# The opening of a fused encoder layer: where a constant part is summed, what stands ahead of the norm's root, and which engine does the sine products

## The chip, the cores and the metric

The kernel runs on one core of a Trainium2 chip. The metric is the device time of one execution in microseconds; less is better. Five engines take part: TensorE (PE in the profile; its weight loads are PEld), VectorE (DVE), ScalarE (ACT), GpSimd (POOL) and SyncE (SP), whose queue issues nearly all the transfers. Each engine works through its own instructions strictly in the order in which they stand; semaphores tie the engines together. A wait at the head of one engine therefore holds everything that is queued behind it there.

## The reference

One layer over 1024 positions of 1024 features, in float32:

```
mod = silu(c) @ w_ada + b_ada
sh1, sc1, g1, sh2, sc2, g2 = split(mod, 6)
h = rms_norm(x, norm_mix_g) * (1 + sc1) + sh1
q_a, k_a, v_a, qk_m, v_m, o_m, gates = split(h @ w_in)
y_attn = axial_gqa_attention(rope(rms_norm(q_a)), rope(rms_norm(k_a)), v_a)
y_mem  = bidirectional_mlstm(silu(conv(qk_m)), v_m, o_m, gates)
x = x + g1 * (concat(y_attn, y_mem) @ w_out)
h = rms_norm(x, norm_ffn_g) * (1 + sc2) + sh2
x = x + g2 * ((silu(h @ w_gate) * (h @ w_up)) @ w_down)
return rms_norm(x, final_norm_g)
```

Attention has 8 query heads of 64 and 2 key heads; the rope turns pairs by cosine and sine tables. The mLSTM has 4 heads of 128 and sixteen gate columns, from which running maxima and sums over all positions are made.

## The kernel before

**Tiles.** Features lie on the partitions: x is eight blocks of 128 x 1024 (`x_t`), cut into two halves of 512 positions. Every large product is done as three matmuls (`mm3`, lines 307 to 310): each operand is split into a rounded part (hi) and the rest (lo), and hi x hi, hi x lo and lo x hi are added. The hi part is made on ScalarE (`whi`, `hh`), the lo part on GpSimd or VectorE (`wlo`, `hl`).

**Who sets the order.** The program is written by a planner (`Clock`): it keeps estimated times of the engines, a heap of pending steps, and chains of steps that wait for flags. Each instruction is emitted when its step comes up, so the order on every engine is a result of these estimates and fixed before the run. The chip then follows that order with its true times.

**The opening.** It runs in these stages:

1. *First batch* (line 670 on): while x arrives, three weight tiles (key, value, first query; `acc0`) are multiplied with x scaled by `sc1` alone, without the norm's root and without the shift. Beside it VectorE multiplies rows of `w_ada` with the conditioning (`ada_load`): eight scale columns first, then eight shift columns a0 to a7. The squares of x are summed, and after step k = 5 the norm's root is made (`rstd_steps`, line 603): a table function on ScalarE, then a correction on VectorE, two halves. `rstd` is copied into PSUM (`ms`) by ScalarE.
2. *Second batch* (line 2046 on): now `h_steps` (line 656) makes h itself: x times root (VectorE), scale and shift (ScalarE), hi (ScalarE), lo (GpSimd). With h, PE does the first token-major tile (gates and v of the mLSTM, `acct`, 272 columns, `chunk_step`) and the second query tile (`query`): half 0, then half 1; in half 1 the query products come after the tile's.
3. *Shift's part.* Key, value and first query lack the shift's product with their weights. `load_again` fetches these weights once more, and `shift_sums` multiplies them with the shift (24 tiny products). When it is there, `shifted` finishes the three tiles on ScalarE.
4. *Ropes.* `rope_steps` (line 706): the swapped rows are moved by four transfers (`swap`), multiplied with the sine table (`rp[1]`) on GpSimd, the tile with the cosine table on VectorE, then added. The key's ones need the roots of the key's squares as well; each query has one group of tiny products for its squares.
5. *Gates* (`gate_steps`, line 926): the gate columns (`gI`) are turned by PE into rows, through log-sigmoid on ScalarE, four scans and some ten row operations on VectorE, exponentials on ScalarE, back into columns by PE (the T products of line 1024), and a last sum (`dexp`, line 1042).

From there on PE works through the other projection tiles (`units`), which are also the filling beside attention. Attention begins when queries and gates are done; its scores are S (line 1104). After it come the mLSTM, the output projection and the feed-forward part, which the change doesn't touch.

**Names in the rows.** `ada`: a column of `w_ada` (128x1024) or half a column (128x512, `ada_late`); `sq<-ms`, `sq<-sq`: the root's steps; `wst`, `whi`, `wlo`: a weight piece as it came, its hi and its lo; `raw_q`: the first batch's tiles as they are finished; `sqk`: squares of such a tile; `sw`: the swapped rows; `rps`: the rope tables; `gs`, `gI`: gate columns; `gt`, `Fr`, `T`, `gB`, `rend`: rows of the gates' chain; `wagain`: the weights fetched again. Big buffers of the pool `bp` (tag `big`) are a ring of five.

Of the kernel before, what the change touches and what calls it, by code (L numbers as in the profile page):

```python
# [20 lines left out]
P = 128  # L21
# [226 lines left out]
def layer_kernel(ctx, tc, xT, c, w_ada, vecs, cons, rope, w_f, w_t0, w_t, w_o, w_gu, w_d, out):  # L248
# [112 lines left out]
    with tc.manual_schedule():  # L361
# [122 lines left out]
        def load_piece():  # L484
# [8 lines left out]
            if isinstance(specs[i][0], str):  # L493
# [3 lines left out]
                  lo=dve if specs[i][3:] == (1,) or i < 6 or start["m", 2] <= i < start["b", 1] else None)  # L497
# [28 lines left out]
        ck.at(3.0, lambda: dve.tensor_scalar(b1, V("b_ada", 8, KT), 1.0, None, op0=OP.add))  # L526
        x_at = [Flag() for _ in range(KT)]
        ada_at = [Flag() for _ in range(16)]
        sq_ok, z_ok = {}, {}
        z_read = [Flag() for _ in range(KT)]  # L530
# [21 lines left out]
        def ada_load(j):  # L552
            t = bp.tile([P, D], F32, tag="big", name="ada")
            ck.chain(dma(t, w_ada[j]), *([*z_ok[7], *sq_ok[7]] if j < 8 else []), lambda: dve.scalar_tensor_tensor(
                t, t, 1.0, PP["cond"], op0=OP.mult, op1=OP.mult, accum_out=modacc[:, 0, j:j + 1]), flag=ada_at[j])
# [62 lines left out]
        def shift_sums():  # L618

            ck.need(y_free, slot("ms").flag())  # L620
            acc, f = psum_tile([P, 3, 2], "ms")
# [17 lines left out]
        wagain, again = {}, {}  # L639

        def load_again():

            gI[0] = stp.tile([P, NJ, 2, 64], F32, tag="x", name="gI", bufs=KT)
            gps.memset(gI[0], 0.0)
            for i in range(3):
                w = wagain[i] = stp.tile([P, S], F32, tag="x", name="wagain", bufs=KT)
                again[i] = ck.chain(dma(w, w_f[i].rearrange("p a b -> p (a b)")), lambda: None)
            for i in range(2):
                rp.append(stp.tile([P, S], F32, tag="x", name="rps", bufs=KT))
                dma(rp[i], rope[i])  # L650
# [5 lines left out]
        def h_steps(n, k, *after):  # L656
# [3 lines left out]
                0.0, *after, sh_ok[k], y_ok[n], z_read[k],  # L660
                lambda: dve.tensor_mul(xs, xs, msp[n][0]),
# [8 lines left out]
        for k in range(KT):  # L670
# [15 lines left out]
            if k == 5:  # L686
# [11 lines left out]
                ck.chain(0.0, *last[-3:], lambda: None, flag=y_free)  # L698

# [6 lines left out]
        def rope_steps(i, accs, raw=None, qg=None):  # L706
# [30 lines left out]
            def swap():  # L737
# [3 lines left out]
                ck.chain(arrive, lambda: gps.tensor_mul(sw, sw, rp[1]), lambda: dve.tensor_mul(qg, qg, rp[0]),  # L741
# [46 lines left out]
            else:  # L788
                ck.chain(0.0, rstd_ok[0], lambda: rooted(0), rstd_ok[1], lambda: rooted(1), shift_ok,
# [1252 lines left out]
        for _ in range(3):  # L2042
            load_piece()
        ck.chain(0.0, *sh_ok, lambda: act.activation(sh2, mod[:, 0:KT, None].to_broadcast([P, KT, 2]), AF.Copy), y_free,
                 load_again)
        accs, tiles = [], []
        for n in range(NH):
# [16 lines left out]
            for k in range(KT):  # L2064
# [4 lines left out]
                elif k % 2:  # L2069
                    load_piece()  # L2070
            for j in range(4 * n, 4 * n + 4):
                chunk_out(0, j, *tiles[j])
            if n:
# [182 lines left out]
```

## Time and profile before

| | us |
|---|---|
| three runs | 1399.79, 1400.19, 1396.09; median 1399.79 |
| the profiled execution | 1401.04 |
| its span, first to last instruction | 1399.2 |
| busy: PE, DVE, ACT, POOL | 1291.9, 1051.6, 674.6, 655.8 |
| mean granted clock of PE | 0.96 |

The page's second part shows the span in 40 slices of 35 us; digits are tenths. These are the rows of PE, of VectorE and of PE's granted clock:

```profile
PE   7799848999999999899798899999999999979997
DVE  7906998977888757777598887666766654898866
PEclk9898869999999999999899899999999999989998
```

The opening is the first six slices. PE is at its least in the sixth (175 to 210 us: 4 tenths, at a clock of 6 tenths), while VectorE is full there; in the third (70 to 105 us) it is the other way round. PE is close to full afterwards.

### The profile page before, as it was taken

Reading aid. Unit: us, or ns where it says so; the run is one execution under the profiler, and the core shown is the slowest. Engines: PE = TensorE matmul, PEld = TensorE weight load, DVE = VectorE, ACT = ScalarE, POOL = GpSimd, SP = SyncE. Lnnn points to the kernel's source line nnn. Section 1 sums busy time; section 2 is a strip of 40 time slices with the busy share of each in tenths; the row PEclk is TensorE's granted clock in tenths of the full one; section 3 lists DMA queues with packets and bytes.
Section 4 is the critical chain, followed back from the end, with each engine's and each line's share of the span. In section 5 each row is a group of like instructions: output and inputs, shape, how many; then the busy total and the mean of one; then the engine's idle time right before and its main releaser. Section 6 shows DMA issues by size and latency. Waiting matters only on the chain.

```text
span 1399.2 us, 19615 instructions
## 1 busy us (share of the span) xinstructions
PE 1291.9 (92%) x6632; PEld 1087.9 (78%) x6640; DVE 1051.6 (75%) x1615; ACT 674.6 (48%) x1217; POOL 655.8 (47%) x545
## 2 busy tenths in 40 slices
PE   7799848999999999899798899999999999979997
PEld 5698637888879888787586688888888887867887
DVE  7906998977888757777598887666766654898866
ACT  6746225666666655454376333323333333444462
POOL 0555724435444335786502255545545455545542
PEclk9898869999999999999899899999999999989998
DMA  9343534333112137833463242323322258733324
GB/s 355 122 164 108 165 118 115 116 110 110 52 54 61 35 112 228 281 124 106 158 200 98 83 158 91 108 104 113 113 96 85 83 175 320 295 83 100 97 64 155
DMA packets 103893, 185.99 MB, mean 133 GB/s; under 512 B 11376, under 2 KB 33136, under 8 KB 103792
## 3 DMA queue, kind: packets, MB, share of 16 engines
q1 hardware_dynamic: 90400, 162.63, 36.4%
q10 hardware_dynamic: 13392, 22.10, 4.1%
q8 instruction: 53, 0.87, 0.3%
q14 instruction: 48, 0.39, 0.1%
HBM read 137.76 MB, written 43.25 MB: 129 GB/s over the span
## 4 chain that ended last, share of the span: by engine, by line
PE 61%; DVE 20%; DMA 6%; issue 5%; ACT 4%; POOL 2%; SPq 1%; DVEq 0%; ACTq 0%; POOLq 0%
PE acc L308 15%; PE acc L309 15%; PE acc L310 15%; PE av L1155 3%; PE T L1136 2%; DVE sst L96 2%; PE S L1104 2%; DVE x L96 2%; DVE y L96 2%; DVE PT L96 2%; DVE ada L96 2%; PE acct L308 2%; PE acct L310 1%; PE acct L309 1%; DVE s L96 1%
## 5 line engine op out<-in xcount | busy, mean ns | idle before, releaser
L96 POOL TENSOR_TENSOR wlo<-wst,whi 128x512 fp32r<-128x512 f32 (+2 forms) x190 | 269.6, 1426 | 343.1 <-ACT whi L96 307.5
L96 ACT ACTIVATE whi<-wst 128x512 fp32r<-128x512 f32 (+2 forms) x219 | 131.1, 605 | 127.5 <-PE acc L310 31.9
L96 POOL TENSOR_SCALAR P<-P,sst 128x1024 f32<-128x1024 f32 x64 | 86.9, 1360 | 158.1 <-DVE sst L96 127.2
L309 PE MATMUL acc<-x,whi 128*128 128x512 f32 x352 | 138.7, 394 | 5.9 <-DVE x L96 5.9
L96 POOL TENSOR_TENSOR wlo<-wr,whi 128x512 fp32r<-128x512 f32 x56 | 77.5, 1385 | 75.4 <-ACT whi L96 74.0
L308 PE MATMUL acc<-whi,wch 128*128 128x512 f32 x244 | 96.5, 395 | 5.3 <-ACT wch L96 5.3
L308 PE MATMUL acc<-hh,whi 128*128 128x512 f32 x224 | 97.0, 433 | 3.4 <-ACT xp L96 1.9
L310 PE MATMUL acc<-whi,wcl 128*128 128x512 f32 x244 | 96.4, 395 | 2.9 <-DVE wcl L96 2.9
L309 PE MATMUL acc<-wlo,wch 128*128 128x512 f32 x244 | 96.4, 395 | 0.1
L96 ACT ACTIVATE P<-S,sst,colq 128x1024 f32<-128x1024 f32 x64 | 77.3, 1207 | 35.2 <-DVE sst L96 33.6
L96 ACT ACTIVATE PT<-T 128x512 fp32r<-128x512 f32 x128 | 71.9, 596 | 40.4 <-PE T L1136 39.8
L309 PE MATMUL acc<-hl,whi 128*128 128x512 f32 x224 | 90.7, 405 | 0.0
L310 PE MATMUL acc<-hh,wlo 128*128 128x512 f32 x224 | 90.6, 404 | 0.0
L96 DVE TENSOR_TENSOR PT<-T,PT 128x512 fp32r<-128x512 f32 x128 | 83.0, 682 | 9.1 <-ACT PT L96 8.7
L96 ACT ACTIVATE whi<-wr 128x512 fp32r<-128x512 f32 x60 | 37.9, 632 | 105.3 <-DVE wr L96 50.4
L308 PE MATMUL acct<-whi,hh 128*128 128x256 f32 (+1 forms) x256 | 79.1, 309 | 10.1 <-ACT hh L96 7.4
L96 DVE TENSOR_TENSOR sg<-acc,sg 128x512 f32<-128x512 f32 x67 | 45.4, 687 | 55.7 <-PE acc L310 55.5
L96 POOL TENSOR_TENSOR wlo<-s,whi 128x512 fp32r<-128x512 f32 x40 | 53.9, 1350 | 67.2 <-ACT whi L96 67.2
L309 PEld LDWEIGHTS acc<-x,whi 128*128 128x128 f32 x352 | 66.8, 190 | 21.0 <-DVE x L96 7.3
L96 DVE TENSOR_REDUCE sst<-S 128x1 f32<-128x1024 f32 x64 | 77.7, 1215 | 5.9 <-PE S L1104 5.9
L96 DVE SCALAR_TENSOR_TENSOR ada<-ada,cond 128x512 f32<-128x512 f32 (+1 forms) x80 | 70.5, 888 | 15.4 <-DMA ada<-in_w_ada_dram 9.5
L96 DVE TENSOR_TENSOR wcl<-wd,wch 128x512 fp32r<-128x512 f32 x50 | 50.7, 1025 | 37.8 <-ACT wch L96 32.1
(472 smaller groups left out, 3815.4 us busy)
## 6 DMA issues: line engine op xcount, KB each, us to landing
wr<-in_w_gu_dram SPq DMA_DIRECT2D x66, 256.0 KB, 2.9
ada<-in_w_ada_dram SPq DMA_DIRECT2D x64, 256.0 KB, 3.1
wd<-in_w_d_dram SPq DMA_DIRECT2D x22, 512.0 KB, 6.7
wst<-in_w_gu_dram SPq DMA_DIRECT2D x34, 256.0 KB, 3.1
wst<-act_d SPq DMA_DIRECT2D x33, 256.0 KB, 4.1
ada<-in_w_ada_dram SPq DMA_DIRECT2D x16, 512.0 KB, 6.9
wst<-in_w_o_dram SPq DMA_DIRECT2D x32, 256.0 KB, 3.3
act_d<-sg ACTq DMA_DIRECT2D x31, 256.0 KB, 2.0
```

What stands on the lines that cost most here:

```text
L96: return fn(*args, **kw)
L308: nc.tensor.matmul(acc, w[0], x[0], start=first, stop=False)
L309: nc.tensor.matmul(acc, w[0], x[1], start=False, stop=False)
L310: nc.tensor.matmul(acc, w[1], x[0], start=False, stop=last)
L1104: nc.tensor.matmul(sp[:, halves(n)], qs[:, j * P:(j + 1) * P], k2[g][m][:, halves(n)], start=m == 0, stop=m == 1)
L1136: nc.tensor.transpose(tp[:, k], Pt[q][:, (4 * b + k) * P:(4 * b + k + 1) * P], ident)
L1155: nc.tensor.matmul(av, va[:, k, h // 4], PT[it][m][:, k], start=(k, m) == (0, 0), stop=(k, m) == (NJ - 1, 1))
```

## The change

The diff has six parts:

- `shift_sums` is called between the two halves of the second batch, in a buffer of tag `acc`; `load_again` fetches the weights into big buffers as soon as the shift's columns are there, and the rope tables have a function of their own, `load_tables`, which waits as before until x is free.
- The shift columns a4 to a7 wait until the norm's root is done (`late`). A throw-away call loads the root's table early (`warm`). The first two x blocks take the root itself, not its copy in PSUM, and each block waits for its shift column only before the step that adds it.
- Weight pieces 6 to 8 are split on VectorE, not on GpSimd.
- The second query's `rope_steps` is set up after half 0, with a flag (`more`) for its second half; ropes, value transposes and gates now come in beside half 1. `gate_steps` is put in ahead of half 1's query products.
- The sine products go from GpSimd to VectorE, for all five ropes; they wait for the tables by a flag (`rp_ok`).
- Half columns of `w_ada` (`ada_late`) are asked for in every step of the second batch, and the second PSUM layout `ps0b` (four buffers for the small tags instead of two) is gone.

```
-                  lo=dve if specs[i][3:] == (1,) or i < 6 or start["m", 2] <= i < start["b", 1] else None)
+                  lo=dve if specs[i][3:] == (1,) or i < 9 or start["m", 2] <= i < start["b", 1] else None)
...
+        warm = stp.tile([P, 1], F32, name="warm")
+        ck.at(7.0, lambda: act.activation(warm, eps, AF.Abs_reciprocal_sqrt, scale=1.0, bias=eps))
...
-            ck.chain(dma(t, w_ada[j]), *([*z_ok[7], *sq_ok[7]] if j < 8 else []), lambda: dve.scalar_tensor_tensor(
+            ck.chain(dma(t, w_ada[j]), *([*z_ok[7], *sq_ok[7]] if j < 8 else []), *([late] if 3 < j < 8 else []), lambda: dve.scalar_tensor_tensor(
...
-            ck.need(y_free, slot("ms").flag())
-            acc, f = psum_tile([P, 3, 2], "ms")
+            ck.need(slot("acc").flag())
+            acc, f = psum_tile([P, 3, 2], "acc")
...
         def load_again():
 
+            for i in range(3):
+                w = wagain[i] = bp.tile([P, S], F32, tag="big", name="wagain")
+                again[i] = ck.chain(dma(w, w_f[i].rearrange("p a b -> p (a b)")), lambda: None)
+
+        def load_tables():
+
             gI[0] = stp.tile([P, NJ, 2, 64], F32, tag="x", name="gI", bufs=KT)
             gps.memset(gI[0], 0.0)
-            for i in range(3):
-                w = wagain[i] = stp.tile([P, S], F32, tag="x", name="wagain", bufs=KT)
-                again[i] = ck.chain(dma(w, w_f[i].rearrange("p a b -> p (a b)")), lambda: None)
             for i in range(2):
                 rp.append(stp.tile([P, S], F32, tag="x", name="rps", bufs=KT))
-                dma(rp[i], rope[i])
+                arrive = dma(rp[i], rope[i])
+            ck.chain(arrive, lambda: None, flag=rp_ok)
...
-                0.0, *after, sh_ok[k], y_ok[n], z_read[k],
-                lambda: dve.tensor_mul(xs, xs, msp[n][0]),
+                0.0, *after, (rstd_ok if k < 2 else y_ok)[n], z_read[k],
+                lambda: dve.tensor_mul(xs, xs, rstd[n] if k < 2 else msp[n][0]), sh_ok[k],
...
+                ck.chain(0.0, *rstd_ok, lambda: None, flag=late)
...
-                ck.chain(arrive, lambda: gps.tensor_mul(sw, sw, rp[1]), lambda: dve.tensor_mul(qg, qg, rp[0]),
+                ck.chain(arrive, rp_ok, lambda: dve.tensor_mul(sw, sw, rp[1]), lambda: dve.tensor_mul(qg, qg, rp[0]),
...
-                ck.chain(0.0, rstd_ok[0], lambda: rooted(0), rstd_ok[1], lambda: rooted(1), shift_ok,
+                ck.chain(0.0, rstd_ok[0], lambda: rooted(0), rstd_ok[1], more, lambda: rooted(1), shift_ok,
...
-        ck.chain(0.0, *sh_ok, lambda: act.activation(sh2, mod[:, 0:KT, None].to_broadcast([P, KT, 2]), AF.Copy), y_free,
-                 load_again)
+        ck.chain(0.0, *sh_ok, lambda: act.activation(sh2, mod[:, 0:KT, None].to_broadcast([P, KT, 2]), AF.Copy), load_again)
+        ck.chain(0.0, y_free, load_tables)
...
+                ada_late()
             for j in range(4 * n, 4 * n + 4):
                 chunk_out(0, j, *tiles[j])
-            if n:
+            if n == 0:
+                more = Flag()
+                rope_steps(1, accs, -1, raw_q[1], more)
+                while not again:
+                    ck.pop()
+                shift_sums()
+            else:
+                ck.chain(0.0, *vo_ok[0], gate_steps)
                 for k in range(KT):
                     query(k)
                     if k % 4 == 3:
                         load_piece()
-        rope_steps(1, accs, -1, raw_q[1])
-        while not again:
-            ck.pop()
-        shift_sums()
-        ck.need(*[f for ring in PP["ring"].values() for f in ring])
-        psum_open("ps0b", {"acc": ("acc", 4), "acct": ("acc", 4), "ms": ("aux", 4), "tr": ("aux", 4), "T": ("aux", 4)})
+                    ada_late()
+                more.set(ck, ck.t)
...
-        ck.chain(0.0, *vo_ok[0], gate_steps)
```

How the planner's order changes is seen at three places. First PE, where the shift's part is summed (`L626` before, `L629` now). Before, these rows follow the last query product of half 1:

```order
L310 MATMUL acc<-hh_229,wlo 128x512
L626 MATMUL ms<-sh_264,wagain 128x2 x24
L308 MATMUL acc<-hh_222,whi 128x512
L309 MATMUL acc<-hl_230,whi 128x512
L310 MATMUL acc<-hh_222,wlo 128x512
L938 MATMUL T<-ident,gI 128x128 x4
L308 MATMUL acc<-hh_223,whi 128x512
L309 MATMUL acc<-hl_231,whi 128x512
L310 MATMUL acc<-hh_223,wlo 128x512
L799 MATMUL tr<-ident,vt 128x128 x8
L938 MATMUL T<-ident,gI 128x128 x4
```

With the change they follow the last query product of half 0, and half 1 of the tile (`acct`) comes behind them:

```order
L308 MATMUL acc<-hh_229,whi 128x512
L309 MATMUL acc<-hl_237,whi 128x512
L310 MATMUL acc<-hh_229,wlo 128x512
L629 MATMUL acc<-sh_264,wagain 128x2 x24
L308 MATMUL acct<-whi,hh_222 128x272
L309 MATMUL acct<-wlo,hh_222 128x272
L310 MATMUL acct<-whi,hl_230 128x272
```

The sums moved ahead of 32 products into `acct` and 8 into `acc`. Behind them there follow, inside those 32, the value transposes (after 6), the key's squares and the first query's group (after 13 more) and the key's second half (after 5 more); the gates' first transposes come after 6 of the 8 query products. Up to the first scores S PE has 136 products into `acc` instead of 138, and VectorE 45 `ada` instructions instead of 35.

Second VectorE at the norm's root. Before, with the eight shift columns (`ada`) around the root's steps (`sq`):

```order
L96 SCALAR_TENSOR_TENSOR ada,modacc<-ada,cond 128x1024 x4
L96 TENSOR_SCALAR sq<-ms 128x512 x2
L96 SCALAR_TENSOR_TENSOR ada,modacc<-ada,cond 128x1024 x3
L96 SCALAR_TENSOR_TENSOR sq<-sq,ms 128x512 x2
L96 SCALAR_TENSOR_TENSOR ada,modacc<-ada,cond 128x1024
L96 SCALAR_TENSOR_TENSOR sq<-sq 128x512 x2
L96 TENSOR_TENSOR vt<-acc,sq 128x512
```

With the change:

```order
L96 SCALAR_TENSOR_TENSOR ada,modacc<-ada,cond 128x1024 x4
L96 TENSOR_TENSOR wlo<-wst,whi 128x544
L96 TENSOR_SCALAR sq<-ms 128x512 x2
L96 TENSOR_TENSOR wlo<-wst,whi 128x512
L96 TENSOR_TENSOR wlo<-wst,whi 128x544
L96 SCALAR_TENSOR_TENSOR sq<-sq,ms 128x512 x2
L96 SCALAR_TENSOR_TENSOR sq<-sq 128x512 x2
L96 TENSOR_TENSOR x_248<-x_248,sq 128x512
L96 TENSOR_TENSOR x_249<-x_249,sq 128x512
L96 TENSOR_TENSOR x_250<-x_250,ms 128x512
L96 SCALAR_TENSOR_TENSOR ada,modacc<-ada,cond 128x1024 x4
```

The late four columns moved behind the first three x blocks, and three weight splits came in.

Third VectorE at the gates. Before, from the last gate columns (`gs`) to the value tile (`va`):

```order
L96 COPY gs<-acct 128x16 x8
L96 COPY shift<-ms 128x3
L96 COPY gI<-gs 128x16x4 x2
L96 CAST maskb<-masks 128x128 x4
L96 TENSOR_SCALAR T_1106<-T,vec 64x512
L96 TENSOR_SCALAR Fr<-T,vec 64x512
L96 TENSOR_SCALAR T_1106<-T,vec 64x512
L96 TENSOR_SCALAR Fr<-T,vec 64x512
L96 SCALAR_TENSOR_TENSOR ada,modacc<-ada,cond 128x512 x2
L96 TENSOR_SCALAR sq<-ms 128x512
L96 TENSOR_TENSOR va<-tr,va 128x8x64 x2
```

With the change, up to the same gate columns (`raw_q_259` is the key, `raw_q_257` the first query):

```order
L96 TENSOR_TENSOR sw<-sw,rps 128x1024
L96 TENSOR_TENSOR raw_q_259<-raw_q_259,sw 128x1024
L96 SCALAR_TENSOR_TENSOR ada,modacc<-ada,cond 128x512
L96 TENSOR_SCALAR colq<-rqv 128x8x2
L96 SCALAR_TENSOR_TENSOR sq<-sq,ms 128x512
L96 TENSOR_TENSOR raw_q_257<-raw_q_257,rps 128x1024
L96 SCALAR_TENSOR_TENSOR ada,modacc<-ada,cond 128x512
L96 COPY gs<-acct 128x16 x4
L96 SCALAR_TENSOR_TENSOR sq<-sq 128x512
L96 TENSOR_TENSOR raw_q_257<-raw_q_257,sw 128x1024
L96 COPY gI<-gs 128x16x4 x2
L96 SCALAR_TENSOR_TENSOR ada,modacc<-ada,cond 128x512
```

Before, the ropes came behind the gates' first rows; now those of the key and the first query, sine products included, stand ahead of them.

More of the change, by code (lines that the diff above doesn't have):

```diff
@@ L529, in layer_kernel @@
         sq_ok, z_ok = {}, {}
+        late = Flag()
         z_read = [Flag() for _ in range(KT)]
@@ L639, in layer_kernel @@
         wagain, again = {}, {}
+        rp_ok = Flag()
         def load_again():
+            for i in range(3):
+                w = wagain[i] = bp.tile([P, S], F32, tag="big", name="wagain")
+                again[i] = ck.chain(dma(w, w_f[i].rearrange("p a b -> p (a b)")), lambda: None)
+        def load_tables():
             gI[0] = stp.tile([P, NJ, 2, 64], F32, tag="x", name="gI", bufs=KT)
             gps.memset(gI[0], 0.0)
-            for i in range(3):
-                w = wagain[i] = stp.tile([P, S], F32, tag="x", name="wagain", bufs=KT)
-                again[i] = ck.chain(dma(w, w_f[i].rearrange("p a b -> p (a b)")), lambda: None)
             for i in range(2):
                 rp.append(stp.tile([P, S], F32, tag="x", name="rps", bufs=KT))
-                dma(rp[i], rope[i])
+                arrive = dma(rp[i], rope[i])
+            ck.chain(arrive, lambda: None, flag=rp_ok)
         acc0 = [[psum_tile([P, HALF], "acc") for _ in range(NH)] for _ in range(3)]
@@ L704, in layer_kernel, with rope_steps @@
         va_ok = [Flag(), Flag()]
-        def rope_steps(i, accs, raw=None, qg=None):
+        def rope_steps(i, accs, raw=None, qg=None, more=FREE):
             is_k = i == 4
```

## The prediction

> **What bounds the kernel now.** I read the busy time by stage first, then who made TensorE (PE) wait, then its rows in order of time. Columns of the stages: start:end, length, busy time (count) of PE, PE's weight loads, VectorE (DVE), ScalarE (ACT), GpSimd (POOL), then PE's granted clock, DMA share, GB/s.
>
> ```profile
> 53.40:80.60 27.20, 19.24 (x111) 17.75 (x111) 15.44 (x26) 23.47 (x38) 22.65 (x18) 0.81 0.00 1
> ...
> 150.90:180.90 30.00, 24.68 (x97) 20.45 (x97) 29.69 (x32) 8.48 (x13) 17.95 (x9) 0.84 0.50 157
> 180.90:209.60 28.70, 14.22 (x49) 11.09 (x50) 26.22 (x43) 8.60 (x12) 8.07 (x6) 0.59 0.39 122
> 209.60:505.00 295.40, 281.20 (x1853) 249.66 (x1851) 250.83 (x439) 190.89 (x335) 126.31 (x96) 0.99 0.27 79
> ```
>
> From 209.6 us on PE is busy 95% at full clock: what comes later starts earlier if this point comes earlier. Before it PE stands still and then runs at a lower clock, while VectorE is full (29.69 of 30.00). The waits from 53 to 210 us (total, times, longest):
>
> ```profile
> PE T L1024 <- ACT T L96: 11.0, 2, 5.8
> PE acct L308 <- ACT hh L96: 7.4, 1, 7.4
> PE T L1042 <- DVE dexp L96: 7.3, 1, 7.3
> PE ms L754 <- ACT sqk L96: 6.4, 1, 6.4
> ```
>
> That is 32.1 us of standing still: 7.4 where the second batch begins (it waits for the root of the norm), 18.3 for the gates' tables, 6.4 for a query's squares. PE's own rows (start, duration, what; a wait in brackets):
>
> ```profile
> 60.91 0.59 PE L308 MATMUL acct<-whi,hh 128*128 128x272 f32 x1 [7.41 <-ACT hh L96]
> ...
> 65.14 0.63 PE L309 MATMUL acc<-hl,whi 128*128 128x512 f32 x1
> ...
> 67.96 0.29 PE L308 MATMUL acct<-whi,hh 128*128 128x272 f32 x1
> ...
> 68.34 0.40 PE L308 MATMUL acc<-hh,whi 128*128 128x512 f32 x1
> ...
> 69.04 0.29 PE L308 MATMUL acct<-whi,hh 128*128 128x272 f32 x1
> ...
> 99.84 8.26 PE L626 MATMUL ms<-sh,wagain 128*128 128x2 f32 x48
> 108.44 0.76 PE L308 MATMUL acc<-hh,whi 128*128 128x512 f32 x1 [0.34 <-DVE shift L96]
> ...
> 120.45 3.63 PE L754 MATMUL ms<-con,sqk 128*128 128x2 f32 x32
> ...
> 209.58 1.98 PE L1104 MATMUL S<-k,qs 128*128 128x512 f32 x8
> ```
>
> A product (three matmuls) takes 0.38 us into acct and 0.70 into acc (67.96, 68.34, 69.04; I use 0.68, their steady pace). After the 7.4 us wait a matmul takes 0.63 instead of 0.40 until about 67.9; after the tiny shift sums it is 0.76 as well. One group of squares (L754, half of its row) takes 1.75. Attention's first scores S start at 209.58: that is the mark I carry through.
>
> **The change, part by part.** *Opening.* These rows make the wait at 60.91:
>
> ```profile
> 41.77 2.38 DVE L96 SCALAR_TENSOR_TENSOR ada<-ada,cond 128x1024 f32<-128x1024 f32 x1
> ...
> 47.44 1.28 DVE L96 TENSOR_SCALAR sq<-ms 128x512 f32<-128x512 f32 x2
> ...
> 48.64 1.21 DVE L96 SCALAR_TENSOR_TENSOR ada<-ada,cond 128x1024 f32<-128x1024 f32 x1
> ...
> 54.41 1.28 DVE L96 SCALAR_TENSOR_TENSOR sq<-sq 128x512 f32<-128x512 f32 x2
> ...
> 57.41 1.86 DVE L96 TENSOR_TENSOR x<-x,ms 128x512 f32<-128x512 f32 x3
> ...
> 44.56 1.28 ACT L96 ACT_TABLE_LOAD   x1 [3.88 <-PE ms L690]
> ...
> 58.12 2.23 ACT L96 ACTIVATE x<-x,mod,sc 128x512 f32<-128x512 f32 x3
> ...
> 60.25 1.65 ACT L96 ACTIVATE hh<-x 128x512 fp32r<-128x512 f32 x3
> ...
> 40.24 5.04 POOL L96 TENSOR_TENSOR wlo<-wst,whi 128x544 fp32r<-128x544 f32 x2 [39.82 <-ACT whi L96]
> ...
> 60.94 18.78 POOL L96 TENSOR_TENSOR hl<-x,hh 128x512 fp32r<-128x512 f32 x15
> ```
>
> VectorE's root ends at 55.7 (54.41 + 1.28). Two of the first four shift columns took about 2.3 us instead of 1.2 while GpSimd split weights (41.77 beside 40.24); with pieces 6 to 8 split on VectorE that is 2.2 less, and one split (0.6, as an x product of that size: 1.86 / 3) more, ahead of the root: its first step goes from 47.4 to 45.9. Behind it four late columns leave (4 x 1.15 = 4.6) and two splits come (1.2), so the 8.25 us from there to the root's end become 4.85: **50.8**. The table load (1.28) is then done long before, in ScalarE's idle time near 8 us, hidden by PE's warm-up products; uncovered it would cost its 1.3. The first two x blocks take the root straight, so x is scaled by 51.5, two affine steps (0.74 each) and the first hh (0.6) end at **53.7**, where PE is just free (60.91 - 7.41 = 53.5).
>
> The gain isn't the whole 7.2: GpSimd's first hl takes 1.25 (18.78 / 15), so PE's third matmul waits 0.9, and three splits (3.8 us) now stand between its third and fourth hl, which costs PE 1.5 at the fourth group. Eight groups of 4 x 0.38 + 0.68 = 2.2 end the first half at 73.8, against 80.6 in the stages: **-6.8**. If the root didn't come earlier, this term is nil; if no producer held PE it is -9.
>
> *Sums between the halves.* Their 8.26 us stay on PE, with the slow matmuls after them (2.5 us), at 73.8 to 82.1. On SyncE's queue the three weight loads go ahead of the stores of v and of the rope tables, behind the second batch's weights; they need buffers that the late columns a4 to a6 free near 56, and have 17 us to land while the DMA engines stand empty (share 0.00). If they landed late, PE would wait there with the whole half queued behind it. The half columns of w_ada that are now fetched in each step of the batch cost VectorE 0.68 each, in a stage where it is busy for 15.44 of 27.20 and then nearly idle. What the new place does: v's transposes, the key's squares and one query's group (about 4 us of PE) come inside the half's 32 products of 0.38, and their VectorE work runs where VectorE idled. PE then reaches the gates' transposes at 82.1 + 2.5 + 12.2 + 4 + 6 x 0.68 = 105. VectorE hands over the gate columns only behind the ropes of key and first query: their 25 instructions, 0.2 to 1.2 us each, start when the shift is there (82.4) and end at 106.5, waits for the swapped rows included. So PE waits 1.5 there, and the gates start only 2 us sooner than now. Queued behind them on VectorE are the ropes of the later queries.
>
> *Gates' tables and sine products.* VectorE and GpSimd now:
>
> ```profile
> 108.24 0.30 DVE L96 COPY gI<-gs 128x64 f32<-128x64 f32 x2
> ...
> 128.43 1.23 DVE L96 TENSOR_TENSOR raw_q<-raw_q,sw 128x1024 f32<-128x1024 f32 x1
> ...
> 132.77 3.38 DVE L96 SCALAR_TENSOR_TENSOR Fr<-Fr,gt 64x1024 f32<-64x1024 f32 x1
> ...
> 136.08 0.68 DVE L96 SCALAR_TENSOR_TENSOR ada<-ada,cond 128x512 f32<-128x512 f32 x1
> ...
> 143.08 0.70 DVE L96 SCALAR_TENSOR_TENSOR ada<-ada,cond 128x512 f32<-128x512 f32 x1
> ...
> 147.05 3.29 DVE L96 TENSOR_TENSOR raw_q<-raw_q,sw 128x1024 f32<-128x1024 f32 x1
> ...
> 150.37 2.28 DVE L96 TENSOR_TENSOR_SCAN T<-Fr,T 32x1024 f32<-32x1024 f32 x1
> ...
> 167.45 4.60 DVE L96 COPY rend<-gB 32x8 f32<-32x8 f32 x2
> ...
> 178.56 1.21 DVE L96 TENSOR_TENSOR Fr<-gB,mprev 64x1024 f32<-64x1024 f32 x1
> ...
> 127.57 1.06 ACT L96 ACTIVATE gt<-gt 64x1024 f32<-64x1024 f32 x1
> ...
> 116.63 2.42 POOL L96 TENSOR_TENSOR sw<-sw,rps 128x1024 f32<-128x1024 f32 x1 [9.35 <-DMA sw<-raw_q]
> ...
> 129.90 5.17 POOL L96 TENSOR_TENSOR sw<-sw,rps 128x1024 f32<-128x1024 f32 x2
> ...
> 166.48 5.55 POOL L96 TENSOR_TENSOR k<-kdup,k 128x1024 fp32r<-128x1024 f32 x2
> ```
>
> From gI (108.24) to the logarithm's end (128.63) it is 20.4 us, broken by the key's roots on ScalarE; those now come first, and three passes of the query, abs, exp, log and two loads (about 12 us behind the transposed gates) put the logarithm's end at 119. From the first Fr (132.77) to the last (179.77) VectorE is full for 47.0. Out of these go the 7.0 from 136.08 to 143.08 (key and first query, done earlier) and what GpSimd's sine products took from VectorE: 2.2 in Fr (3.38 beside 129.90's row), 2.1 at 147.05 (clean: 1.23, at 128.43) and about 1.5 later, 5.8 in all; one sine product (1.2) comes in. 47.0 - 7.0 - 5.8 + 1.2 = 35.4: the last Fr ends at 119 + 35.4 = **154.5** instead of 179.8. PE gets there with 55 products (37.4), three groups (5.3) and 1 from 106.5, at 150.
>
> What remains collides still: two 32x8 copies took 4.60 beside 166.48's row. Without any collision the stretch is 28 us: four scans of 2.28, eleven operations of 1.2, six half columns of 0.68, some 2 of small ones. That is the lower end; the upper end, 10 us over mine, has each GpSimd subtraction left there hold VectorE for all its time.
>
> The Trainium skill, "SBUF — State Buffer", section "Who interferes with whom", has it that a VectorE operation with two SBUF inputs and a GpSimd one that reads SBUF exclude each other for a whole instruction. By that rule the moved products only change who waits, and five splits (1.25) and two key subtractions (2.8) would hold VectorE some 12 us above the clean 28: the last Fr at 159, and a sum 4.5 us higher, inside the forecast's own range. The trace agrees as far as 167.45 beside 166.48 goes.
>
> From the last Fr to S it is now 209.6 - 179.8 = 29.8, with two waits on the way (the second T and dexp). Six products now stand between the columns and dexp's sum, eleven behind it instead of ten: I take 26 (bounds 23 and 30). S starts at 180.5: **-29.1** (of which the opening is 6.8). By then two projection products fewer are done (136 against 138): **+1.4**. Without the second PSUM layout the transposes share two buffers instead of four until attention: that parts the T transposes by a product each, and is inside the 23 to 30. Ten more half columns (45 against 35, 0.68 each) are done before the first scores and leave attention's VectorE; PE binds there, so I count nothing.
>
> **Sum.** The profiled execution took 1401.04 us (span 1399.2), 0.1% over the median shown, 1399.79. 1401.0 - 29.1 + 1.4 = **1373 us**.
>
> **Rivals.** *No collisions:* the last Fr at 147; PE's own work binds (150, S at 169): 1362. *VectorE stays the wall:* the remaining GpSimd work, or gate columns queued longer behind the ropes, make Fr 10 us later: 1383; for it speaks that VectorE is full in 150.90 to 180.90, against it the 7.0 that moved. *Only the opening gains,* the gates wait as long as before: 1394. *Given back later:* attention's 295 us are VectorE's, so that S's lead is lost: 1401; against it 281.20 of PE beside 250.83. *Slower, the wait moves with the product:* GpSimd waited 9.35 us for the swapped rows (116.63) and nobody minded; VectorE waits in order, with gate columns and scans queued behind. Five such waits are 47 us: 1420. It decides from 5.5 us a product (27.7 / 5). Against it: four swaps are issued in 2.5 us and land some 2 later, and the order leaves more work than that between. That the table is loaded again before the root can be excluded: the order has no load there.
>
> **How the numbers follow.** Forecast (1366 to 1381) 0.60; no collisions (1358 to 1366) 0.10; VectorE the wall (1381 to 1390) 0.12; only the opening 0.06; given back 0.05; slower 0.07. The range takes the first three: 1358 to 1391. A measurement here tells 0.3% (4 us) from no change: faster 0.88, same 0.05, slower 0.07.
>
> **What would show it.** PE's first acct at 53.5 to 54.5 with a wait under 1.5 us; the shift sums' row at 73 to 75; gI at 105 to 109; the log's end near 119; the last Fr at 147 to 164, S at 170 to 190, and PE's busy share after S unchanged. Wrong if VectorE waits for a DMA at a sine product for over 5 us, if the weights land after 74, or if attention lasts over 305 us.

## The result, and the profile after

| | before | changed |
|---|---|---|
| median of four runs each, us | 1399.0 | 1408.95 |
| lowest to highest | 1396.09 to 1400.19 | 1407.23 to 1413.44 |
| profiled execution, us | 1401.04 | 1413.44 |
| its span | 1399.2 | 1411.7 |

The ratio is 1.0079, with a 95% interval of 1.005 to 1.0109: the change makes the kernel slower by 0.8%, some 11 us, where 1373 us and a gain of 2% were forecast. The profiled execution is the slowest of the four; the sums below are made against its own span, as the prediction did.

The 40 slices of the page of the changed kernel, PE, VectorE and PE's clock, show the outline. Each slice is 35.3 us here.

```profile
PE   7799779999999993989799799999999999979997
DVE  7948989977888634888598897666766654998876
PEclk9889879999999996999899899999999999989999
```

The hole that the sixth slice had before (PE at 4 tenths) has filled to 7. A new one stands in the sixteenth (529 to 565 us): PE at 3 tenths with its clock at 6, and VectorE at 4. There attention is over and the mLSTM has begun.

The stages say how much. Columns as in the prediction's first block. First of before, then of the changed kernel: from the first scores S to attention's last product, from there to the feed-forward part, and the rest.

```profile
209.60:513.50 303.90, 289.70 (x1923) 258.02 (x1921) 254.55 (x445) 195.97 (x345) 127.89 (x98) 0.99 0.27 80
513.50:761.40 247.90, 226.00 (x1175) 189.76 (x1183) 180.17 (x369) 137.77 (x303) 134.12 (x164) 0.96 0.55 175
761.40:1399.20 637.80, 608.32 (x2758) 502.11 (x2756) 468.18 (x570) 238.01 (x408) 301.99 (x222) 0.97 0.39 129
```

```profile
197.70:511.90 314.20, 300.57 (x1990) 269.66 (x1991) 255.44 (x431) 198.32 (x352) 128.36 (x101) 0.98 0.23 70
511.90:773.50 261.60, 218.44 (x1113) 181.20 (x1120) 185.74 (x370) 135.90 (x299) 126.70 (x160) 0.93 0.52 164
773.50:1411.70 638.20, 608.16 (x2758) 501.48 (x2757) 468.41 (x569) 237.72 (x408) 301.52 (x222) 0.98 0.38 129
```

S comes 11.9 us earlier (197.7 against 209.6). Attention then takes 10.3 us longer and the stage behind it 13.7, while PE is busy there for 7.6 less; the feed-forward part is the same within 0.4. So -11.9 + 10.3 + 13.7 + 0.4 = +12.5 us, the difference of the spans. The 10.3 is work and no loss in itself: the first matmul of a projection product (line 308) occurs 237 times in this stretch instead of 214, and PE is busy for 10.9 us more. These are the two views that count it, before and changed (the number in brackets):

```profile
209.60:513.60 304.00, 76.79 (x214) 0.99 0.27 80
```

```profile
197.70:511.90 314.20, 83.66 (x237) 0.98 0.23 70
```

Before the change, two of the 23 were done ahead of S and 21 behind attention; there 43 are left instead of 64. From S to the feed-forward part the changed kernel takes 24.0 us longer; PE is busy for 3.3 of these and stands still for 20.7. What was lost stands in the list of who waited, PE in the whole span:

```profile
PE U L1865 <- DVE Cs L96: 21.4, 1, 21.4
PE acct L308 <- DVE vt L96: 9.9, 2, 8.8
```

Two waits, neither of them in the prediction. The large one first: PE at the first head's states U of the mLSTM, with VectorE beside it (timeline of the changed kernel, PE, then VectorE).

```profile
559.24 2.07 PE L1865 MATMUL U<-wv,kt 128*128 128x260 f32 x4 [21.44 <-DVE Cs L96]
```

```profile
541.48 0.82 DVE L96 SCALAR_TENSOR_TENSOR ada<-ada,cond 128x512 f32<-128x512 f32 x1 [1.89 <-DMA ada<-in_w_ada_dram]
...
548.64 0.69 DVE L96 SCALAR_TENSOR_TENSOR ada<-ada,cond 128x512 f32<-128x512 f32 x1 [1.27 <-DMA ada<-in_w_ada_dram]
...
557.85 0.69 DVE L96 SCALAR_TENSOR_TENSOR ada<-ada,cond 128x512 f32<-128x512 f32 x1 [1.58 <-DMA ada<-in_w_ada_dram]
...
558.75 0.81 DVE L96 SCALAR_TENSOR_TENSOR Cs<-Cs,dec,U 128x130 f32<-128x130 f32 x2
```

VectorE works off twelve half columns of `w_ada` in a row, from 535.6 to 558.5, and waits for the transfer of nearly every one: two buffers are there, so at most two transfers are under way, and one half column comes every 1.9 us. The two small Cs steps for which PE waits are queued behind them. The code explains why they stand in one block: 48 of the 64 half columns are asked for up to the end of attention; the other 16 are asked for beside the mLSTM's steps, as long as projection products last; when those are over, a loop (`while not summed`) fetches whatever is left, and only then goes on with the mLSTM. I call this block the flush; it is covered while PE has projection products beside it, and bare when it has none. Before, the 16 half columns lay between 521.7 and 565.5, under projection products of which the last starts at 558.6. Now the last one starts at 535.6. These groups (shortest, middle and longest duration in ns, first and last start) show it: the half columns before, the products before, the products of the changed kernel.

```profile
L96 DVE SCALAR_TENSOR_TENSOR ada<-ada,cond x16: 674/689/1754, 521.7 to 565.5; 128x512 f32<-128x512 f32 x16
L310 PE MATMUL acct<-whi,hl x123: 278/283/288, 439.7 to 558.6; 128*128 128x256 f32 x123
```

```profile
L310 PE MATMUL acct<-whi,hl x116: 278/283/285, 440.1 to 535.6; 128*128 128x256 f32 x116
```

The smaller wait is in the opening (VectorE, then PE, changed kernel):

```profile
49.52 1.29 DVE L96 SCALAR_TENSOR_TENSOR sq<-sq 128x512 f32<-128x512 f32 x2
...
52.53 1.22 DVE L96 SCALAR_TENSOR_TENSOR ada<-ada,cond 128x1024 f32<-128x1024 f32 x1
53.67 2.31 DVE L96 SCALAR_TENSOR_TENSOR ada<-ada,cond 128x1024 f32<-128x1024 f32 x1
55.91 2.27 DVE L96 SCALAR_TENSOR_TENSOR ada<-ada,cond 128x1024 f32<-128x1024 f32 x1
58.11 2.28 DVE L96 SCALAR_TENSOR_TENSOR ada<-ada,cond 128x1024 f32<-128x1024 f32 x1
60.32 0.68 DVE L96 TENSOR_TENSOR vt<-acc,sq 128x512 f32<-128x512 f32 x1
```

```profile
61.14 0.57 PE L308 MATMUL acct<-whi,hh 128*128 128x272 f32 x1 [8.80 <-DVE vt L96]
...
83.19 7.62 PE L629 MATMUL acc<-sh,wagain 128*128 128x2 f32 x48
```

The root ends at 50.81, and the second batch could begin at 53.5. But its accumulators are PSUM buffers of tag `acc`, and all six are still held by the first batch, until VectorE has taken them out (`vt`, of the value tile, and `raw_q`). The four late columns, which wait for the root and no longer, are queued ahead of these copies: PE starts at 61.14, later than the 60.91 of before.

### The profile page after: what moved, and what is told of

It is laid out like the page before. It is cut to its first block, busy times and chain, and to the rows that moved or that the text cites. A ratio compares the mean times of both kernels' runs of the same rounds, so it can differ in the third digit from the quotient of the medians.

```text
span 1411.7 us, 19611 instructions
## 1 busy us (share of the span) xinstructions
PE 1291.5 (91%) x6632; PEld 1087.6 (77%) x6640; DVE 1068.9 (76%) x1623; ACT 673.2 (48%) x1217; POOL 634.4 (45%) x537
## 3 DMA queue, kind: packets, MB, share of 16 engines
q1 hardware_dynamic: 90400, 162.63, 36.1%
## 4 chain that ended last, share of the span: by engine, by line
PE 63%; DVE 22%; issue 5%; DMA 4%; ACT 3%; POOL 2%; SPq 0%; ACTq 0%; DVEq 0%; POOLq 0%
PE acc L310 16%; PE acc L309 16%; PE acc L308 16%; PE av L1164 3%; DVE sst L96 3%; DVE ada L96 3%; DVE y L96 3%; PE T L1145 2%; PE S L1113 2%; DVE PT L96 2%; DVE x L96 2%; PE acct L308 2%; PE acct L309 1%; PE acct L310 1%; DMA ada<-in_w_ada_dram 1%
## 5 line engine op out<-in xcount | busy, mean ns | idle before, releaser
L96 POOL TENSOR_TENSOR wlo<-wst,whi 128x512 fp32r<-128x512 f32 (+2 forms) x187 | 264.3, 1420 | 297.3 <-ACT whi L96 266.7
L96 ACT ACTIVATE whi<-wst 128x512 fp32r<-128x512 f32 (+2 forms) x219 | 130.9, 605 | 106.2 <-PE acc L310 32.9
L96 POOL TENSOR_SCALAR P<-P,sst 128x1024 f32<-128x1024 f32 x64 | 81.8, 1279 | 163.8 <-DVE sst L96 136.8
L96 DVE SCALAR_TENSOR_TENSOR ada<-ada,cond 128x512 f32<-128x512 f32 (+1 forms) x80 | 81.4, 1029 | 21.4 <-DMA ada<-in_w_ada_dram 13.0
L96 DVE TENSOR_TENSOR PT<-T,PT 128x512 fp32r<-128x512 f32 x128 | 83.5, 683 | 13.8 <-ACT PT L96 13.4
L96 DVE TENSOR_TENSOR sg<-acc,sg 128x512 f32<-128x512 f32 x67 | 45.4, 687 | 55.7 <-PE acc L310 55.5
```

The costliest lines, as they stand in the source:

```text
L96: return fn(*args, **kw)
```

## The experiments

Every time below goes with the kernel before, run on the same chip; "us" beside a ratio is the ratio times 1400. The traces of all of them, by stage (count: projection products in attention; U: PE's wait at the mLSTM's states):

| | S starts | S to attention's end (count) | from there to the feed-forward part | U |
|---|---|---|---|---|
| before | 209.6 | 303.9 (214) | 247.9 | 0 |
| changed | 197.7 | 314.2 (237) | 261.6 | 21.4 |
| columns early | 195.7 | 303.9 (205) | 255.8 | 0 |
| copies first | 192.6 | 311.3 (237) | 262.3 | 21.9 |
| both | 194.1 | 305.3 (205) | 253.7 | 0 |
| before, columns early | 207.4 | 311.3 (224) | 241.4 | 1.1 |
| before, columns bare | 206.1 | 304.5 (214) | 266.2 | 21.6 |
| four buffers | 195.3 | 310.8 (237) | 250.9 | 12.1 |
| sine on GpSimd | 203.7 | 311.1 (237) | 259.6 | 20.8 |
| second layout | 198.9 | 320.2 (235) | 261.4 | 20.7 |
| 60 columns | 194.1 | 308.2 (221) | 252.1 | 0 |
| 52 columns | 194.3 | 301.3 (200) | 249.5 | 1.0 |
| four buffers, split | 195.4 | 312.9 (223) | 257.2 | 3.9 |
| both, split | 190.3 | 313.0 (218) | 248.8 | 0 |

Each row is one execution. Several of these kernels have the same order up to S, so their S should be the same, and it isn't quite: 206.1 to 209.6 (before and its two variants), 195.3 to 197.7 (changed, columns early, four buffers), 192.6 to 194.3 (copies first, both, 60 and 52 columns), 190.3 and 195.4 (the two with the split). Differences of S below some 4 us, with the split 5 us, say nothing.

**Columns early.** The changed kernel with no half column left for the mLSTM (the sum over the last columns is set up earlier in the text for it):

```
-        def ada_late(last=48, ahead=2):
+        def ada_late(last=64, ahead=2):
```

> The changed kernel, but all 64 half columns of w_ada may be fetched before the mLSTM, where so far only 48 may and 16 wait for it. Theory (bare flush): the changed kernel loses its lead in the 21.4 us for which PE waits at the mLSTM's first U products, because the projection products run out there and the 12 half columns left are worked off back to back, with nothing beside them. Without them the wait is gone: 1409 - 21 = 1388 us (1384 to 1391), no wait over 3 us of PE at U. Rival (VectorE): the sixteen half columns, 0.68 each, now lengthen attention by up to 11 us: 1398 to 1400. Second rival (the mLSTM's own start is slow): PE waits at U for the states all the same, over 10 us, and the time stays over 1400.

1395.34 us, ratio 0.9957 (0.9932 to 0.9981): 17 us under the changed kernel's ratio. The wait at U is gone, and the kernel is now faster than before. The second rival falls: nothing waits at U. The median is under the 1398 of the first, too, but its mechanism is not excluded: attention takes 303.9 us as before, with nine products fewer. The 21 us didn't come whole. The count in attention changed with the edit (205 instead of 237), so this run alone doesn't part the flush from the order; the two further down, with the count unchanged, do.

**Copies first.** The late columns wait for the six accumulators:

```
-                ck.chain(0.0, *rstd_ok, lambda: None, flag=late)
+                ck.chain(0.0, *[f for a in acc0 for _, f in a], lambda: None, flag=late)
```

> The changed kernel, but the shift columns a4 to a7 wait until the first batch's six accumulators have been copied out of PSUM, not only until the root is done. Theory (buffers): PE's first acct product waits (8.8 us, until 61.1) for VectorE's copies, which free the accumulators and stand behind the four late columns; with the copies ahead it starts at 54.5 to 56.5, the shift sums at 75 to 79 instead of 83.2, S 4 to 6 us earlier, and the whole takes 1403 to 1405 us. Rival (products): x products and hl, not the buffers, hold the half; the first acct comes earlier but the shift sums start at 81 to 83 and the time stays at 1409.

1405.7 us, ratio 1.0041 (1.0026 to 1.0056), 5 us less by the medians; the two intervals just overlap. PE's rows that wait in the second batch, and the shift sums:

```profile
53.23 0.39 PE L308 MATMUL acct<-whi,hh 128*128 128x272 f32 x1 [0.91 <-ACT hh L96]
...
66.15 0.59 PE L310 MATMUL acct<-whi,hl 128*128 128x272 f32 x1 [3.16 <-POOL hl L96]
...
78.34 5.80 PE L629 MATMUL acc<-sh,wagain 128*128 128x2 f32 x46
```

The first product starts at 53.23, under the 54.5 that I gave it and half a microsecond ahead of the prediction's 53.7; the sums start 4.9 us earlier and S 5.1, of which the groups of S above bear out 2.5 (means 193.8 and 196.2). So the buffers held the half. It still doesn't reach 73.8: the three splits on GpSimd, ahead of the fourth hl, take 6.91 us and cost PE 3.2, and VectorE's late columns take 2.3 us each beside GpSimd.

**Both edits.**

> Both edits of the two runs beside it. If the two losses are independent, as the theories have it, the gains add: 21 + 5 below the changed kernel, 1383 us (1379 to 1387). Rival: what the opening gains is lost again at the gates, where VectorE is the wall: as the run with the columns early alone, 1388.

1394.5 us, ratio 0.9947 (0.9929 to 0.9965): 18.5 us under the changed kernel, where the two apart make 17 and 5. S came at 194.1; the order up to it is that of copies first, so the 1.5 us between the two are scatter. The time is nearly that of the columns early alone, as the rival has it, and the sum of the two would be a ratio of 0.9919, just under the interval; but that sum is made of three uncertain ratios, and the run doesn't decide between theory and rival.

**The kernel before with the columns early**, the same line:

> The kernel before, with the same one edit: all 64 half columns may come before the mLSTM. Theory (bare flush): before, the flush is covered by projection products but for 5.5 us of PE's idle time between 558.8 and 566.2, so it gains 3 to 7: 1392 to 1396 us. Rival (VectorE in attention): slower than before, up to 1410. Rival (the edit is worth as much everywhere, so that it says nothing of the change): 1378.

1402.5 us, ratio 1.002 (1.0008 to 1.0033). My theory's number is wrong, and the rival holds: slower. Attention and the stage behind it:

```profile
207.40:518.70 311.30, 295.60 (x1952) 263.26 (x1951) 269.74 (x479) 197.77 (x348) 131.61 (x101) 0.99 0.31 93
518.70:760.10 241.40, 220.82 (x1146) 182.71 (x1154) 171.65 (x335) 137.15 (x299) 125.01 (x160) 0.98 0.50 161
```

VectorE is busy in attention for 15.2 us more than before (269.74 against 254.55). Attention takes 7.4 longer, with ten products more (4.7 of it, at the 10.9 / 23 of above), and the stage behind it gives back 6.5. This profiled execution is the fastest of its ten (1399.37), so its rows can't show where the others lose 3 us; that it is VectorE in attention remains the rival's argument. What the run does show: the same edit gains nothing where the flush is covered.

**The kernel before with the flush made bare.** The 16 columns are no longer asked for beside the mLSTM's steps:

```
-        ck.tick = lambda: ada_late(64)
+        ck.tick = None
```

> The kernel before, with the last 16 half columns of w_ada no longer asked for beside the mLSTM's steps: they are all fetched when the projection products are over. The amount of projection work left at each point stays as before. Theory (bare flush): the loss of the changed kernel is made in the kernel before. Twelve half columns took 21.4 us there, 1.8 each; sixteen take 28, less the 5.5 for which PE stands still there already: 1399 + 16 to 24 = 1415 to 1423 us, with one wait of PE of 18 to 28 us behind a Cs step of VectorE. Rival (it is the lack of projection work beside the mLSTM, not the flush): within 5 us of before.

1416.67 us, ratio 1.0123 (1.0104 to 1.0142): 17 us slower, with the projection products where they were (214 in attention). The wait is there, in the kernel before:

```profile
PE U L1856 <- DVE Cs L96: 21.6, 2, 20.3
```

This is the cause made by hand: nothing of the opening was touched.

**Four buffers for the flush.** Now the cause is made smaller, in the changed kernel, with the order otherwise as it was:

```
-        ck.tick = lambda: ada_late(64)
+        ck.tick = lambda: ada_late(64, 4)
...
-            ck.need(*adas[-2:])
-            ada_late(64)
+            ck.need(*(adas[-4:-3] if len(adas) < 64 else adas[-2:]))
+            ada_late(64, 4)
```

> The changed kernel, with four buffers instead of two for the last 16 half columns; the rest of the order is the same. Theory (paced by latency): two buffers let two transfers be under way, and each pair takes 3.4 to 3.9 us; with four the twelve come in 10 to 14 us instead of 21.4, and the time is 7 to 11 us less: 1398 to 1402. Rival (paced by bandwidth or by the queue): 1.5 us or more each as now; wait of 18 to 22, time 1406 to 1410.

1400.35 us, ratio 0.9997 (0.9981 to 1.0013), 11 us less, and the wait at U is 12.1, with the count in attention unchanged. That a shorter flush gives time back is shown. Why it is shorter has two parts: when the projection products ended, nine half columns were left instead of twelve, and they came every 1.5 us (13.5 us in all) instead of every 1.9. So the pace is the 1.5 that the rival named, though the wait and the time are the theory's. With four buffers a transfer took longer: of those issued from 526 to 531, five took 3.8 to 5.4 us from issue to landing, against 2.5 to 3.2 in the changed kernel's block from 539 on. Three of VectorE's rows also took 1.74 us instead of 0.69 beside GpSimd's splits. The time of a single transfer alone doesn't set the pace.

**Sine products on GpSimd again**, the one engine name in `swap` put back.

> The changed kernel with the five sine products on GpSimd again. The prediction's step: the product on GpSimd took 5.8 us from VectorE's rows and saves it 1.2, so VectorE's last Fr and the first scores S come 4 to 5 us later than 169.3 and 197.7, and the time is 1412 to 1414. Rival (even): VectorE loses in the products what it gains in the other rows, S within 1.5 us, 1407 to 1411. Second rival: VectorE was waiting there for swapped rows, S comes earlier, 1403 to 1406.

1414.54 us, ratio 1.0106 (1.0084 to 1.0129): 4 us slower than the changed kernel by the medians, with intervals that overlap; S comes 6.0 us later, more than S scatters by. For S that step of the prediction holds; for the whole time it is likely and not shown. Two of VectorE's scans in this run, GpSimd beside them, and then one scan of the changed kernel:

```profile
136.79 6.58 DVE L96 TENSOR_TENSOR_SCAN T<-Fr,T 32x1024 f32<-32x1024 f32 x2
```

```profile
136.91 4.32 POOL L96 TENSOR_TENSOR sw<-sw,rps 128x1024 f32<-128x1024 f32 x1
141.19 5.51 POOL L96 TENSOR_TENSOR wlo<-wst,whi 128x512 fp32r<-128x512 f32 x2
```

```profile
137.98 2.27 DVE L96 TENSOR_TENSOR_SCAN T<-Fr,T 32x1024 f32<-32x1024 f32 x1
```

Each scan takes 3.3 us beside sine product and splits, 2.3 in the changed kernel.

**The second PSUM layout kept** (the two removed lines of the diff put back behind the second batch).

> The changed kernel with the second PSUM layout kept (four buffers for the small tags, from the end of the second batch on). Theory: PE's 6.8 us at a T product, for VectorE's cols copies, are the price of two buffers instead of four; they go, S comes 4 to 7 us earlier and the time is 1402 to 1405. Rival: PE waits for dexp in their place, as before the change (7.3 us), S within 2 us, 1407 to 1411.

1420.81 us, ratio 1.0158 (1.0135 to 1.0181): 11 us slower than the changed kernel, which neither theory gives. The 6.8 us for cols are gone; waits for T (4.3, twice) and dexp (2.6) stand in their place, and S is 1.2 us later, within its scatter. As the prediction had it, the layout was worth nothing up to S. Of the 7.1 us between the two spans 6.0 are lost in attention, with two products fewer; PE's waits there for the transposed attention weights (PT), in this kernel, and in the changed one:

```profile
PE T L1145 <- DVE PT L96: 12.2, 19, 2.3
```

```profile
PE T L1145 <- DVE PT L96: 6.8, 12, 2.5
```

The order of the projection products in attention is another one, and it meets VectorE worse. What in that order does it stays open.

**Columns moved in part.** Both of these have the copies first, four buffers, and 60 or 52 half columns before the mLSTM:

```
-        def ada_late(last=48, ahead=2):
+        def ada_late(last=60, ahead=2):
```

> The changed kernel with the accumulators' copies ahead of the late columns, 60 half columns before the mLSTM instead of 48 and four buffers for the rest; by the order, 9 us of projection products more are left when attention ends than in the kernel with all columns early. Theory (bare flush, nothing else): no wait over 3 us at U; S as in the run with the copies first (193), the rest as with the columns early: 1388 to 1394 us. Rival (more projection work left beside the mLSTM costs time by itself): over 1397.

> As the run before, with 52 half columns before the mLSTM; more projection work is left for the mLSTM (21 us at its first step instead of 11), and four half columns are left after that. Theory: still no wait over 3 us at U, 1388 to 1394. Rival (projection work beside the mLSTM costs time by itself): slower than the run with 60 by 3 us or more.

With 60: 1393.29 us, ratio 0.9932 (0.9915 to 0.995). With 52: 1387.52 us, ratio **0.9895** (0.9868 to 0.9922), the fastest of all: 26 us under the changed kernel and 15 under before. My rival said that more projection work beside the mLSTM costs time; by the medians the run with more of it is the faster one, and the two intervals hardly overlap. Its stages:

```profile
194.30:495.60 301.30, 286.36 (x1880) 254.17 (x1880) 258.14 (x442) 196.57 (x342) 126.55 (x97) 0.99 0.24 72
495.60:745.10 249.50, 231.01 (x1221) 193.32 (x1230) 180.03 (x361) 139.97 (x306) 134.22 (x164) 0.99 0.54 174
```

From S to the feed-forward part it takes 550.8 us, as before the change (551.8): here, and only here, S's lead of 15.3 us arrives at the end whole (the span is 14.7 shorter).

**Weight pieces 9 to 11 split on VectorE too**, with the copies first, and four buffers in the one run, all columns early in the other:

```
-                  lo=dve if specs[i][3:] == (1,) or i < 9 or start["m", 2] <= i < start["b", 1] else None)
+                  lo=dve if specs[i][3:] == (1,) or i < 12 or start["m", 2] <= i < start["b", 1] else None)
```

> The changed kernel with the copies ahead of the late columns, four buffers for the last 16 half columns, and weight pieces 9 to 11 split on VectorE too (they stand on GpSimd between the third and the fourth hl, and PE waited 3.2 us for that). Theory: that wait goes, the shift sums start 2 to 3 us earlier than 78.3 to 79.3; the order leaves 4.4 us more projection work after attention and spreads the half columns, so the wait at U is under 6 us: 1390 to 1396. Rival: VectorE pays for the splits in the x products, shift sums no earlier; or the wait at U stays at 12: 1397 to 1400.

> The kernel with both repairs (all columns early, copies first) and pieces 9 to 11 split on VectorE. Theory: PE's 3.2 us wait for hl goes, shift sums at 76 to 77.5, S at 190 to 192, total 1390 to 1393. Rival: VectorE is the wall from there to S, S no earlier than 193: 1394 to 1397.

Four buffers and split: 1400.31 us, ratio 0.9988 (0.9969 to 1.0006), at the rival's end of the forecast, with the wait at U that the theory gave. Both and split: 1392.64 us, ratio 0.9939 (0.9922 to 0.9957), the sums, S and the time as the theory had them, but no different from both without the split. PE's wait of 3.2 us for hl went to 1.0 and 0.9, but PE waits for hh in its place (2.8 and 1.7): the sums start at 78.75 and 77.16. In the second run S comes at 190.3 (195.4 in the first, with the same order up to there) and attention takes 7.7 us longer than without the split, with 13 products more in it. In the first the half columns are spread out beside the mLSTM, the wait at U falls to 3.9, and yet the stage takes 257.2: of what PE waits for there, 6.6 us are for yah, the first operand of the output projection, and the run with 52 columns has no such wait over 1 us; but the changed kernel (6.3) and 60 columns (6.4) have it too, so it doesn't set this run apart. Removing the wait at U isn't the whole cure there, and I haven't taken that apart.

## Why the prediction was wrong

**The step that failed most: everything behind S was taken as unchanged.** The prediction took 1189.6 + 1.4 = 1191.0 us from S to the end; it was 1214.0, 23.0 more. It argued that PE binds from S on, so that S's lead passes through, and that the half columns done early count nothing. PE does bind in attention: by and large a run's time there goes with its count of products (301.3 with 200, 310.8 to 314.2 with 237; the second layout, 320.2 with 235, and both with the split, 313.0 with 218, lie off). But the lead is only kept if PE also has work at the seam, where attention ends and the mLSTM begins. There the order had 21 products fewer left, against the same 16 half columns, because the limit of 48 stops them whether they start early or not. The cover of the flush went, and 21.4 us of it came into the open. Two runs carry this: the flush made bare in the kernel before costs 17 us, and four buffers take 9.3 us off the wait and 11 off the time. That the missing products are the reason why it lay bare is read from the counts and from where the products end (535.6 against 558.6). Two pairs agree with it and are no clean tests: four buffers with 237 products in attention wait 12.1 and with 223 wait 3.9, but the second has another opening; and the run with 52 columns, 200 products and a wait of 1.0 also has fewer half columns left. Why the order put more products into attention stays open: among the kernels with the copies first the count went from 237 with 48 half columns to 200 with 52, 221 with 60 and 205 with 64.

**The opening, -6.8.** "Where PE is just free" was the wrong half of the sentence. Root (50.8 predicted, 50.81 measured) and first hh (53.7, 53.54) came as worked out; PE was free, its accumulators were not. I counted what leaves the stretch ahead of the root on VectorE, and not what the removed work is now ahead of. The sums started 9.4 us late. With the copies first the start is right, and the half still ends at 78.3 instead of 73.8: the term is then -2.3, not -6.8. Its wait for the fourth hl was under-sized (1.5, and 3.16 measured: the three splits took 6.91 and not 3.8), and the matmuls from 55.5 to 58.8 ran at 0.43 us instead of 0.29 there.

**The gates.** These rows carry the chain from the gate columns on (changed kernel, VectorE; ScalarE's logarithm ended at 130.9):

```profile
117.04 0.28 DVE L96 COPY gI<-gs 128x64 f32<-128x64 f32 x2
...
132.25 2.30 DVE L96 SCALAR_TENSOR_TENSOR Fr<-Fr,gt 64x1024 f32<-64x1024 f32 x1
...
151.85 3.30 DVE L96 TENSOR_TENSOR sw<-sw,rps 128x1024 f32<-128x1024 f32 x1
...
155.19 3.43 DVE L96 COPY mprev<-T 32x7 f32<-32x7 f32 x2
...
168.07 1.21 DVE L96 TENSOR_TENSOR Fr<-gB,mprev 64x1024 f32<-64x1024 f32 x1
```

gI stood at 106.5 in the prediction: 9.4 of the 10.5 late are the opening's. From gI to the logarithm 13.8 were measured and 12.5 predicted; from there to the last Fr 38.4 and 35.4 (two rows beside GpSimd still take 3.3 and 3.4); from Fr to S 28.4 and 26, inside the bounds. So S is late by 9.4 + 1.1 + 1.3 + 3.0 + 2.4 = 17.2. The mechanisms up to Fr are right, with sizes short; the last part stayed inside its bounds partly by luck, for the wait for dexp is gone and PE waits 6.8 us for the gates' columns that VectorE copies (`cols`), which the prediction didn't have. All these sizes are short by 8 in sum, and the opening was wrong. One reading of the prediction is off as well: it takes the copies at 167.45 for a case of a VectorE operation with two inputs held up by GpSimd, but a copy has one input. Its row at 132.77, with two inputs and 3.38 us beside GpSimd's, is nearer to that.

**What was right.** The weights for the sums were there (their row waits for nothing). The sine products on VectorE bring S 6.0 us forward, where 4.6 was worked out (5.8 less 1.2), and VectorE waited at most 1.0 for a swapped row: the slower rival that I gave 0.07 isn't what happened. The second layout was worth nothing up to S. The two products fewer by S are there. Of the rivals, "given back later" (1401) and "slower" (1420) have the times on either side; neither mechanism, attention bound by VectorE or waits for swapped rows, is the one found.

**The sum.** 17.2 at S and 23.0 behind it are 40.2 us, which but for rounding is the 1413.4 of the profiled execution over the 1373.3 (1401.0 - 29.1 + 1.4).

**What stays open.** With the flush gone, the runs with the columns early, both, 60 columns, and both with the split still need 559 to 562 us from S to the feed-forward part, before and the run with 52 columns 551 to 552. In three of the four, waiting is the smaller part of these some 8 us. PE is busy there for 521.0 us (columns early), 522.1 (both), 519.4 (60 columns) and 524.6 (both, split), against 515.7 before, of which the two products more behind S (four with the split) are 1.4 (2.8); it stands still for 38.7, 36.9, 40.9 and 37.2, against 36.1. Why nearly the same matmuls keep PE busy for longer I haven't found.

## What to carry to other kernels

A lead at one point of a PE-bound kernel is worth what covers the next seam: before counting it through to the end, list the work that must be done at each pool's or stage's close, and count what is left in the order to lie over it, before and after. When work is taken from ahead of a stretch on an in-order engine, look at what it now stands in front of, and for each product of the next stage at who still holds its accumulators. And where small transfers must come in a row through a few buffers, count how many will be left when the cover ends: here twelve took 22.9 us through two buffers, and nine took 13.5 through four.

## What the runs showed of the hardware

- Half columns (256 KB each) through two buffers came every 1.9 us with nothing else on VectorE; with four buffers every 1.5 us, while a transfer then took up to 5.4 us to land instead of 2.5 to 3.2.
- Where VectorE and GpSimd met, sometimes the one paid and sometimes the other. In the changed kernel the scan at 137.98 kept its 2.27 us, and two of GpSimd's splits beside it took 5.14 (two took 2.52 at 118.89); at 155.19 two copies of no more than 32 x 7 elements took 3.43 beside a subtraction of GpSimd's. The length of such a row says little about what it can lose.
- The same program scattered by up to 11 us from run to run where half columns had been moved (columns early: 1387.6 to 1398.48 in seven runs), while before stayed within 6 (1396.51 to 1402.13 in seventeen). Why is not known. Within one order, S itself came at 190.3 in one execution and at 195.4 in another.
